# Narrow matmuls for the first modulation rows, another spread of the later ones, and the R loads on ScalarE's queue

## The chip, the core and the metric

The kernel runs on one core of a Trainium2 chip. A core has five engines, each of which executes its own instructions in order: TensorE (PE, with its weight loads as PEld), VectorE (DVE), ScalarE (ACT), GpSimd (POOL) and SyncE (SP), which here issues nearly all DMA transfers. An engine that meets an instruction whose inputs are not there waits, and everything behind it on that engine waits too. The metric is the device time of one execution in microseconds.

## The reference

One layer of a diffusion backbone with 128 context tokens and 2048 latent tokens, model width 1024. What matters here:

```python
shift1, scale1, gate1, shift2, scale2, gate2 = split(silu(c) @ w_mod + b_mod, 6)
h = rmsnorm(x, norm1) * (1 + scale1) + shift1
z = h @ w_in                      # conv parts, q, k, v, o and 16 gate columns
h_m = mlstm_bidir(q, k, v, gates, C0, n0, m0)      # chunks of 128 tokens, both directions
h_m = rmsnorm_per_head(h_m) * mh_norm * sigmoid(o)
x = x + gate1 * (concat(y_shortconv, h_m) @ w_out)
h2 = rmsnorm(x, norm2) * (1 + scale2) + shift2
x = x + gate2 * (ffn(h2) @ w_down)
```

The modulation is a vector of 6 x 1024 numbers for each of two conditionings (context and latent tokens), so w_mod is a 1024 x 6144 matrix that is multiplied by two columns. Shift1 and scale1 (the first 2048 numbers) are needed before any product of the layer; the other four parts are needed later.

## The kernel before

Data are kept transposed, 128 channels on the partitions and tokens along the free axis. Every large fp32 product is made of three matmuls: each operand x is split into a rounded part xH and a rest xL, and wh\*xH, wl\*xH and wh\*xL are accumulated. The split of a weight block costs one ScalarE copy (L112) and two VectorE subtractions (L115), for a block loaded by L110 into one of two buffers `wst`; the split of activations costs one ScalarE copy (L594) and one VectorE subtraction (L595) per tile.

A framework's scheduler turns the program into one instruction list per engine. It takes the instructions roughly in the order in which the code emits them and moves those that it expects to be ready sooner; so the place of a call in the code sets, within bounds, its place on each engine. Pools of a few buffers delay a load until the last user of the buffer is done.

The stages that the change touches:

- **Opening (0 to about 98 us).** `mod_pe` (L619 to L630) computes one row of 128 modulation numbers on TensorE: it loads a 512 KB block of w_mod (L625) into a free buffer of the tiles wsu or xg, multiplies it in 8 matmuls by the two conditioning columns, repeated to 128 columns (L628), and VectorE adds the bias to the first two columns (L630). `mods` does two rows (scale and shift) per 128 channels and then forms the factor `ab` (L120). `raws(0)` loads the first 512 latent tokens, `gsquares` (L582 to L591) adds up their squares (ScalarE L589, VectorE L590), `inv_rms` (L123 to L133) makes the inverse root mean square (TensorE L129, VectorE L132, GpSimd L133), `spread` (L140) copies it over the partitions, and `gapply` (L597 to L602) scales and shifts each tile (VectorE L600, ScalarE L601) and splits it. Then come the products of v and the gate columns, called vg (TensorE L397 to L399, evictions L402 and L404), 24 matmuls for each accumulator; there are four accumulator banks. `second` is the same for the next 512 tokens ("block 1") and runs beside the vg products of the first.
- **Pairs and first products (98 to 340 us)**, untouched.
- **Side rows.** The other 32 modulation rows are computed by VectorE: `mod_dve` loads a row block `wm` (L892) and does two multiply-and-sum instructions per row (L896) and one addition (L897). It is a generator that is advanced once at chosen places: at every second step of the vg products of the remaining tokens (loop L1204 to L1207), two rows for each step of the gate phase and each pair of k products (L1210 to L1219), at every second step of the woven sums (`weave`, L1184 to L1203), and the rest in a run behind them. The memory of `wm` is then given to the Mix units.
- **Gate phase (about 393 to 442 us).** `gate_phase` (L945 to L1033) turns the gate columns into decays: copies (L950), a minimum (L954, tile fe), exp and ln on ScalarE (L955, L956, each with a table load), a subtraction (L957, tile fc), transposes on TensorE (L964), scans over the tokens on VectorE (L914 to L939), and the transposed columns (L1001, TensorE L1003). The matmuls of the k heads (L216 to L218) run beside it.
- **Sums and Mix (about 440 to 960 us).** `weave` runs 34 units of the backward sums, then 34 units `Mix` (outputs), each a little beside large products as fill. A Mix unit loads R, a row of 1024 numbers broadcast to 128 partitions (512 KB, L1110, four buffers), adds the mask (VectorE L1122), takes exp (ScalarE L1126), makes the products (TensorE L1121, L1144, L1146; VectorE L1129, L1130), normalises (VectorE L1150 to L1154, ScalarE L1163 and L1167, TensorE L1173) and stores the gated result o (VectorE L1175, SP L1178). `out_proj` beside it loads rows of x (L485), multiplies by w_out, adds (VectorE L502), stores (L504) and squares (ScalarE L516, VectorE L517).
- Then the up and down products run until the end, on instruction lists that the change leaves alone.

Of the kernel before, what the change touches and what calls it, by code (L numbers as in the profile page):

```python
# [10 lines left out]
F32 = mybir.dt.float32  # L11
F32R = mybir.dt.float32r
AF = mybir.ActivationFunctionType
# [5 lines left out]
P = 128  # L19
# [24 lines left out]
def bc(ap, shape):  # L44
    return ap.to_broadcast(shape)
# [13 lines left out]
def hymba_kernel(ctx: ExitStack, tc: tile.TileContext, I, O):  # L59
    nc = tc.nc  # L60
    V, S, G, PE, Q = nc.vector, nc.scalar, nc.gpsimd, nc.tensor, nc.sync
# [30 lines left out]
    csil = cst.tile([P, KT, 2], F32, name="csil")  # L92
# [8 lines left out]
    ssp = ctx.enter_context(tc.tile_pool(name="ssp", bufs=2))  # L101

    def run(g, side=None, every=1):
        for i, _ in enumerate(g):
            if side and i % every == 0:
                next(side, None)
# [28 lines left out]
    def spread(r, n):  # L135

        ps = pst.tile([P, 512], F32, name="st")
        for i in range((n + P - 1) // P):
            w = min(P, n - i * P)
            PE.matmul(ps[:, i * P:i * P + w], bc(r[:w, i:i + 1], [w, P]), ident[:w, :w], start=True, stop=True)  # L140
        return ps
# [63 lines left out]
    def accumulator():  # L205
        pool = pa[next(turn_a) % len(pa)]
        return pool.tile([P, 512], F32, name="acc")
# [157 lines left out]
    with ExitStack() as ph1:  # L365
# [4 lines left out]
        sqp = ph1.enter_context(tc.tile_pool(name="sqp", bufs=2))  # L370
# [179 lines left out]
        with tc.tile_pool(name="ex", bufs=1, side="right") as ex, \  # L550
# [27 lines left out]
            def gcol(blk):  # L578
                c = TG // P + 4 * blk
                return rc[:, c:c + 4]  # L580

            def gsquares(xr):  # L582
                ss = ssp.tile([P, 512], F32, name="ss")
                for k, x in enumerate(xr):
                    if k == 0:
                        S.activation(ss, x, AF.Square)
                        continue
                    sq = sqp.tile([P, 512], F32, name="sq")
                    S.activation(sq, x, AF.Square)  # L589
                    V.tensor_add(ss, ss, sq)  # L590
                return ss  # L591

            def put(x, to):
                S.activation(to[0], x, AF.Copy)  # L594
                V.tensor_sub(to[1], x, to[0].bitcast(F32))  # L595

            def gapply(blk, xr):  # L597
                rb = spread(gcol(blk), NG)
                for k, x in enumerate(xr):
                    V.scalar_tensor_tensor(x, x, ab[:, 0, k, 1:2], rb[:, :NG], op0=ALU.mult, op1=ALU.mult)  # L600
                    S.activation(x, x, AF.Identity, bias=modT[:, k, 1:2])  # L601
                    put(x, plain[blk][k])  # L602
                    yield
# [16 lines left out]
            def mod_pe(mt):  # L620
                if next(homes6) == "u":
                    st = ex.tile([P, WN], F32, name="wsu", bufs=2)
                else:
                    st = xg.tile([P, 2, NG], F32, name="xg", bufs=4).rearrange("p k t -> p (k t)")
                Q.dma_start(st[:, :D], I["w_mod"][mt])  # L625
                ps = accumulator()
                for k in range(KT):
                    PE.matmul(ps[:, :P], st[:, k * P:(k + 1) * P], bc(csil[:, k, None, :], [P, 64, 2]),  # L628
                              start=(k == 0), stop=(k == KT - 1))
                V.tensor_scalar(modT[:, mt, :], ps[:, :2], bmod[:, mt:mt + 1], None, op0=ALU.add)  # L630

            def mods(k0, k1):
                for k in range(k0, k1):
                    mod_pe(8 + k)
                    mod_pe(k)
                    affine(0, k, k + 1)
# [6 lines left out]
            Q.dma_start(ident, I["ident"])  # L643
            mods(1, 2)
            x1 = raws(0)
            ss = gsquares(x1)
            mods(2, 4)
            ws = load_vg(0)
            inv_rms(ss, NG, gcol(0))
            mods(4, 8)  # L650
            run(gapply(0, x1))
            ws += load_vg(1)
            Q.dma_start(bgate, I["b_gate"].to_broadcast([P, 16]))
            x2 = raws(1)

            def second():
                ss = gsquares(x2)
                yield
                inv_rms(ss, NG, gcol(1))
                yield  # L660
                yield from gapply(1, x2)
# [5 lines left out]
            side = second()  # L667
# [6 lines left out]
            side = gsums(x1, x2)  # L674
# [187 lines left out]
            side = chain(first_stats(), prep_down())  # L862
# [39 lines left out]
        side = mod_dve()  # L902
# [194 lines left out]
        class Mix:  # L1097
# [6 lines left out]
            def load(self):  # L1104
                c, hp = self.c, self.hp
                self.k2, self.v2 = load2(ml, "k2", kD, c + 1, hp), load_v(c + 1, hp)
                self.q2 = load2(mb, "q2", qD, c + 1, hp)
                self.R = mb.tile([P, 2, 2, 2, P], F32, name="R", bufs=4)
                r0 = (c + 1) * H + 2 * hp
                Q.dma_start(self.R.rearrange("p h k d t -> p (h k d t)"),  # L1110
                            nD[r0:r0 + 2].rearrange("h k d t -> (h k d t)")[None, :].to_broadcast([P, 1024]))
                if c >= 0:
                    self.sb = ml.tile([P, 2, 2, 129], F32, name="sb", bufs=5)
                    Q.dma_start(self.sb, sD[hp, c])
# [65 lines left out]
        def weave(units, fill, blocks, lead, side=None):  # L1180

            n = len(units)
            for i in range(-1, n + 3):
                if 0 <= i < n:  # L1184
                    units[i].first()
                if 0 <= i - 3 < n:
                    units[i - 3].third()
                if 0 <= i - 1 < n:
                    units[i - 1].second()
                for x in range(lead) if i < 0 else (i + lead,):  # L1190
                    if x < n:
                        units[x].load()
                for _ in range(blocks[i % 3]):
                    next(fill, None)
                if side and i % 2:
                    next(side, None)


# [4 lines left out]

        for x, _ in enumerate(vg_first()):  # L1204
            next(third, None)
            if x % 2:
                next(side, None)  # L1207
        run(third)
        with tc.tile_pool(name="gt", bufs=1, side="right") as gt:
            gph = gate_phase()  # L1210
            kh = heads(BA, hs, 16, kD, AF.Copy, 1.0)
            while True:
                try:
                    next(gph)
                except StopIteration as e:
                    cols, colc, decB = e.value
                    break
                run(islice(kh, 2), side, 2)
            run(kh, side, 2)  # L1219
        sbs, sfs = [], []  # L1220
        for hp in range(2):
            sb = ml.tile([P, 2, 2, 129], F32, name="sb", bufs=5)
# [31 lines left out]
        side = sums(0, fpool, (0,), (6,))  # L1254
# [16 lines left out]
    with ph2:  # L1271
# [141 lines left out]
        side = sums(1, fpool)  # L1413
# [77 lines left out]
        for w, (hf, x) in enumerate(PRODS):  # L1491
            n = HN[hf] // 2 // NP[hf]
            for mp, ps in units_of(w):
                acc = {p: bank(next(turn))[:, :n] for p in ps}
                for c, nk in enumerate(KS):
# [4 lines left out]
                    for p in ps:  # L1500
                        for kk in range(nk):
                            k = slice(kk * P, (kk + 1) * P)
                            t = slice((NP[hf] * kk + p) * n, (NP[hf] * kk + p + 1) * n)
# [8 lines left out]
                    if jobs and jobs[0][0] + 1 <= step:  # L1512
                        k, ch = jobs[0]
# [93 lines left out]
```

## Time and profile before

| | |
|---|---|
| time, median of 3 runs | 2476.62 us (2476.61 to 2480.12) |
| profiled execution | 2481.01 us, of which the span is 2479.2 |
| TensorE busy | 2427.5 us (98%) |
| VectorE, ScalarE, GpSimd busy | 1806.6, 1146.3, 65.4 us |
| memory traffic | 506.08 MB, 204 GB/s mean |
| mean granted TensorE clock | 0.991 |

A row of a timeline has the start, the time, the engine, the line, the operation with its output and inputs, and in brackets the idle time of the engine before it and what ended that. A window's row has the busy time of each engine in that stretch and the granted clock of TensorE (1.00 is full). Lines are those of the kernel before; in the changed kernel the lines of the opening are one lower, and those from the side rows on are seven higher (L628 is L627, L896 is L903, L1110 is L1117).

### The profile page before, as it was taken

The numbers are of one execution on the slowest core, as the hardware profiler recorded it, in microseconds if no ns is written. First come the engines' busy times: TensorE is split into PE (matmuls) and PEld (weight loads), VectorE is DVE, ScalarE is ACT, GpSimd is POOL, SyncE is SP. The second block draws the span as 40 slices with busy tenths as digits, with TensorE's granted clock in tenths as the row PEclk, the third lists the DMA queues.
The fourth block names the chain that finished last, engine by engine and source line by source line (L and its number), as shares of the span: only waits on it lengthen the run. The fifth ranks groups of instructions, "written<-read, shape, count | busy, mean of one in ns | idle before, by whom it ended". The sixth has DMA issues, their size and how long they took to land.

```text
span 2479.2 us, 42907 instructions
## 1 busy us (share of the span) xinstructions
PE 2427.5 (98%) x16347; PEld 2322.7 (94%) x16347; DVE 1806.6 (73%) x3419; ACT 1146.3 (46%) x2166; POOL 65.4 (3%) x127
## 2 busy tenths in 40 slices
PE   8999999999999999999999999999999999999998
PEld 7987889989999989999999999999999988889998
DVE  4767678862567776888798879776767787677665
ACT  4533453352344444465454446555545554543343
POOL 0000000000101110000000000000000000000000
PEclk9999999999999999999999999999999999999999
DMA  7457557787567886966465446544444486576444
GB/s 287 129 191 256 206 191 223 234 257 217 163 190 232 280 249 197 302 233 234 143 229 195 164 143 240 185 149 161 138 161 145 164 292 221 201 275 208 173 155 149
DMA packets 249119, 506.08 MB, mean 204 GB/s; under 512 B 22722, under 2 KB 143698, under 8 KB 238034
## 3 DMA queue, kind: packets, MB, share of 16 engines
q1 hardware_dynamic: 248914, 503.35, 61.0%
q8 instruction: 128, 2.10, 0.4%
q14 instruction: 77, 0.63, 0.1%
HBM read 355.24 MB, written 148.03 MB: 203 GB/s over the span
## 4 chain that ended last, share of the span: by engine, by line
PE 78%; DMA 11%; DVE 7%; issue 2%; ACT 1%; SPq 1%; POOL 0%; DVEq 0%; ACTq 0%; POOLq 0%
PE pa L1446 7%; PE pa L1448 7%; PE pa L1447 7%; PE acc L216 4%; PE acc L218 4%; PE acc L217 4%; PE pb L1448 3%; PE pb L1446 3%; PE pb L1447 3%; PE pa L1505 2%; PE pa L1504 2%; PE pa L1506 2%; PE pc L1446 2%; PE pc L1448 2%; PE pc L1447 2%; DMA wm<-in_w_modr 2%
## 5 line engine op out<-in xcount | busy, mean ns | idle before, releaser
L1446 PE MATMUL pa<-tH,wh 128*128 128x272 f32 x1408 | 409.1, 291 | 3.1 <-DVE row L502 2.3
L1448 PE MATMUL pa<-tH,wl 128*128 128x272 f32 x1408 | 408.3, 290 | 0.0
L1447 PE MATMUL pa<-tL,wh 128*128 128x272 f32 x1408 | 406.3, 289 | 0.3 <-DVE tL L283 0.3
L289 ACT ACTIVATE wh<-st 128x512 fp32r<-128x512 f32 (+1 forms) x312 | 189.5, 609 | 412.8 <-PE pa L1447 117.2
L216 PE MATMUL acc<-hH,wh 128*128 128x384 f32 (+1 forms) x960 | 330.4, 344 | 0.0
L218 PE MATMUL acc<-hH,wl 128*128 128x384 f32 (+1 forms) x960 | 322.0, 335 | 0.0
L217 PE MATMUL acc<-hL,wh 128*128 128x384 f32 (+1 forms) x960 | 321.2, 335 | 0.0
L1287 DVE SCALAR_TENSOR_TENSOR tt<-raw,fw,tt 128x127 f32<-128x127 f32 (+4 forms) x264 | 242.3, 948 | 43.5 <-ACT tt L1293 42.3
L290 DVE TENSOR_TENSOR wl<-st,wh 128x512 fp32r<-128x512 f32 (+1 forms) x312 | 205.4, 661 | 92.8 <-ACT wh L289 88.9
L1446 PEld LDWEIGHTS pa<-tH,wh 128*128 128x128 f32 x1408 | 265.9, 189 | 3.9 <-DVE row L502 2.4
L1447 PEld LDWEIGHTS pa<-tL,wh 128*128 128x128 f32 x1408 | 266.7, 189 | 0.5 <-DVE tL L283 0.5
L1448 PEld LDWEIGHTS pa<-tH,wl 128*128 128x128 f32 x1408 | 265.6, 189 | 0.0
L1446 PE MATMUL pb<-tH,wh 128*128 128x272 f32 x704 | 204.0, 290 | 1.9 <-ACT tH L282 1.1
L1448 PE MATMUL pb<-tH,wl 128*128 128x272 f32 x704 | 203.8, 290 | 0.0
L1447 PE MATMUL pb<-tL,wh 128*128 128x272 f32 x704 | 202.9, 288 | 0.0
L216 PEld LDWEIGHTS acc<-hH,wh 128*128 128x128 f32 x960 | 182.0, 190 | 1.4 <-issue 0.4
L217 PEld LDWEIGHTS acc<-hL,wh 128*128 128x128 f32 x960 | 181.7, 189 | 0.8
L218 PEld LDWEIGHTS acc<-hH,wl 128*128 128x128 f32 x960 | 181.5, 189 | 0.4 <-issue 0.2
L289 ACT ACTIVATE wh<-s 128x512 fp32r<-128x512 f32 x176 | 110.9, 630 | 150.5 <-PE pc L1447 90.5
L290 DVE TENSOR_TENSOR wl<-s,wh 128x512 fp32r<-128x512 f32 x176 | 120.8, 687 | 32.1 <-ACT wh L289 28.3
L1446 PEld LDWEIGHTS pb<-tH,wh 128*128 128x128 f32 x704 | 132.6, 188 | 2.5 <-ACT tH L282 1.3
L1447 PEld LDWEIGHTS pb<-tL,wh 128*128 128x128 f32 x704 | 132.9, 189 | 0.1
(301 smaller groups left out, 5931.9 us busy)
## 6 DMA issues: line engine op xcount, KB each, us to landing
st<-in_w_up SPq DMA_DIRECT2D x88, 512.0 KB, 4.7
wU<-s SPq DMA_DIRECT2D x22, 1024.0 KB, 7.6
s<-wU SPq DMA_DIRECT2D x22, 1024.0 KB, 5.5
st<-wD SPq DMA_DIRECT2D x32, 704.0 KB, 4.2
st<-in_w_down SPq DMA_DIRECT2D x28, 704.0 KB, 4.2
wst<-in_w_in SPq DMA_DIRECT2D x38, 512.0 KB, 4.6
R<-nD SPq DMA_DIRECT2D x34, 512.0 KB, 5.0
wm<-in_w_modr SPq DMA_DIRECT2D x32, 512.0 KB, 4.9
```

The lines of the kernel that those rows point to most:

```text
L216: PE.matmul(acc[:, :n], w_h, hH[:, k, :n], start=(k == 0), stop=False)
L217: PE.matmul(acc[:, :n], w_h, hL[:, k, :n], start=False, stop=False)
L218: mm = PE.matmul(acc[:, :n], w_l, hH[:, k, :n], start=False, stop=(k == KT - 1))
L289: S.activation(wh[:, :n], a, AF.Copy)
L290: V.tensor_sub(wl[:, :n], a, wh[:, :n].bitcast(F32))
L1287: V.scalar_tensor_tensor(o, i, w, o, op0=ALU.mult, op1=ALU.add)
L1446: PE.matmul(acc, wh[:, w], rh, start=(kk == 0 and i in (0, 1, 5)), stop=False, skip_group_check=True)
L1447: PE.matmul(acc, wh[:, w], rl, start=False, stop=False, skip_group_check=True)
L1448: mm = PE.matmul(acc, wl[:, w], rh, start=False, stop=(kk == 3), skip_group_check=True)
L1504: PE.matmul(acc[p], wh[:, k], th[:, t], start=(c == kk == 0), stop=False, skip_group_check=True)
L1505: PE.matmul(acc[p], wh[:, k], tl[:, t], start=False, stop=False, skip_group_check=True)
L1506: PE.matmul(acc[p], wl[:, k], th[:, t], start=False, stop=(c == 2 and kk == nk - 1), skip_group_check=True)
```

## The change

Four edits:

1. The modulation matmuls move 32 columns instead of 128. The first two of them are used, as before.
2. `gsquares` becomes a generator. The squares of the first block are spread over modulation steps 2 to 4, the weights of vg are loaded and the inverse root follows, and `gapply(0)` is spread over steps 6 and 7.
3. R is loaded by ScalarE's DMA queue instead of SP's.
4. Side rows: 7 beside the vg products, none beside the gate phase and the k products, and in the woven sums at three of four steps instead of every second.

```diff
--- before.py
+++ after.py
@@ -579,16 +579,15 @@
                 c = TG // P + 4 * blk
                 return rc[:, c:c + 4]
 
-            def gsquares(xr):
-                ss = ssp.tile([P, 512], F32, name="ss")
+            def gsquares(xr, ss):
                 for k, x in enumerate(xr):
                     if k == 0:
                         S.activation(ss, x, AF.Square)
-                        continue
-                    sq = sqp.tile([P, 512], F32, name="sq")
-                    S.activation(sq, x, AF.Square)
-                    V.tensor_add(ss, ss, sq)
-                return ss
+                    else:
+                        sq = sqp.tile([P, 512], F32, name="sq")
+                        S.activation(sq, x, AF.Square)
+                        V.tensor_add(ss, ss, sq)
+                    yield
 
             def put(x, to):
                 S.activation(to[0], x, AF.Copy)
@@ -625,7 +624,7 @@
                 Q.dma_start(st[:, :D], I["w_mod"][mt])
                 ps = accumulator()
                 for k in range(KT):
-                    PE.matmul(ps[:, :P], st[:, k * P:(k + 1) * P], bc(csil[:, k, None, :], [P, 64, 2]),
+                    PE.matmul(ps[:, :32], st[:, k * P:(k + 1) * P], bc(csil[:, k, None, :], [P, 16, 2]),
                               start=(k == 0), stop=(k == KT - 1))
                 V.tensor_scalar(modT[:, mt, :], ps[:, :2], bmod[:, mt:mt + 1], None, op0=ALU.add)
 
@@ -643,18 +642,26 @@
             Q.dma_start(ident, I["ident"])
             mods(1, 2)
             x1 = raws(0)
-            ss = gsquares(x1)
-            mods(2, 4)
+            ss = ssp.tile([P, 512], F32, name="ss")
+            sq = gsquares(x1, ss)
+            for k in range(2, 5):
+                mods(k, k + 1)
+                run(islice(sq, 3))
             ws = load_vg(0)
             inv_rms(ss, NG, gcol(0))
-            mods(4, 8)
-            run(gapply(0, x1))
+            mods(5, 6)
+            ap = gapply(0, x1)
+            for k in range(6, 8):
+                run(islice(ap, 3))
+                mods(k, k + 1)
+            run(ap)
             ws += load_vg(1)
             Q.dma_start(bgate, I["b_gate"].to_broadcast([P, 16]))
             x2 = raws(1)
 
             def second():
-                ss = gsquares(x2)
+                ss = ssp.tile([P, 512], F32, name="ss")
+                run(gsquares(x2, ss))
                 yield
                 inv_rms(ss, NG, gcol(1))
                 yield
@@ -1107,7 +1114,7 @@
                 self.q2 = load2(mb, "q2", qD, c + 1, hp)
                 self.R = mb.tile([P, 2, 2, 2, P], F32, name="R", bufs=4)
                 r0 = (c + 1) * H + 2 * hp
-                Q.dma_start(self.R.rearrange("p h k d t -> p (h k d t)"),
+                S.dma_start(self.R.rearrange("p h k d t -> p (h k d t)"),
                             nD[r0:r0 + 2].rearrange("h k d t -> (h k d t)")[None, :].to_broadcast([P, 1024]))
                 if c >= 0:
                     self.sb = ml.tile([P, 2, 2, 129], F32, name="sb", bufs=5)
@@ -1192,7 +1199,7 @@
                         units[x].load()
                 for _ in range(blocks[i % 3]):
                     next(fill, None)
-                if side and i % 2:
+                if side and i % 4:
                     next(side, None)
 
 
@@ -1203,7 +1210,7 @@
 
         for x, _ in enumerate(vg_first()):
             next(third, None)
-            if x % 2:
+            if x < 14 and x % 2:
                 next(side, None)
         run(third)
         with tc.tile_pool(name="gt", bufs=1, side="right") as gt:
@@ -1215,8 +1222,8 @@
                 except StopIteration as e:
                     cols, colc, decB = e.value
                     break
-                run(islice(kh, 2), side, 2)
-            run(kh, side, 2)
+                run(islice(kh, 2))
+            run(kh)
         sbs, sfs = [], []
         for hp in range(2):
             sb = ml.tile([P, 2, 2, 129], F32, name="sb", bufs=5)
```

Three places show how this moves the instruction lists. First TensorE in the opening (L628/L627 modulation rows, L129 and L140 the inverse root and its spread, L397 to L399 vg), before:

```order
L628 MATMUL acc<-csil,wsu 128x128 x16
L628 MATMUL acc<-csil,xg 128x128 x32
L628 MATMUL acc<-csil,wsu 128x128 x16
L129 MATMUL st<-ones,ss 128x1 x4
L628 MATMUL acc<-csil,xg 128x128 x32
L628 MATMUL acc<-csil,wsu 128x128 x16
L628 MATMUL acc<-csil,xg 128x128 x16
L140 MATMUL st<-ident,rc 128x128 x4
L397 MATMUL acc<-wh,hH 128x264
```

and of the change:

```order
L627 MATMUL acc<-csil,xg 128x32 x8
L140 MATMUL st<-ident,rc 128x128 x2
L627 MATMUL acc<-csil,wsu 128x32 x8
L140 MATMUL st<-ident,rc 128x128 x2
L627 MATMUL acc<-csil,wsu 128x32 x8
L627 MATMUL acc<-csil,xg 128x32 x32
L627 MATMUL acc<-csil,wsu 128x32 x8
L397 MATMUL acc<-wh,hH 128x264
L398 MATMUL acc<-wl,hH 128x264
L399 MATMUL acc<-wh,hL 128x264
```

The spread of block 0 stands between rows 6 and 8 instead of behind all 16, and vg begins behind 13 rows; the other three rows stand between vg matmuls. Block 1's L140 has 115 vg matmuls ahead of it before, and 127 now.

Second VectorE ahead of the gate phase, from the eviction (L404) that runs at 391.67 us in the profile before (L896/L903 and L897/L904 are a side row, L115 the weight split, L954/L961 makes fe, L957/L964 fc). Before:

```order
L404 TENSOR_TENSOR gates<-acc,bgate 128x8
L896 SCALAR_TENSOR_TENSOR wm,mt<-wm,cB 128x1024
L950 COPY ic<-gates 128x64
L950 COPY fc<-gates 128x64
L897 TENSOR_SCALAR modT<-mt,bmod 128x2
L115 TENSOR_TENSOR wl<-wst,wh 128x512 x2
L896 SCALAR_TENSOR_TENSOR wm,mt<-wm,cB 128x1024
L404 TENSOR_TENSOR gates<-acc,bgate 128x8
L896 SCALAR_TENSOR_TENSOR wm,mt<-wm,cB 128x1024
L115 TENSOR_TENSOR wl<-wst,wh 128x512
```

and of the change:

```order
L404 TENSOR_TENSOR gates<-acc,bgate 128x8
L115 TENSOR_TENSOR wl<-wst,wh 128x512
L957 COPY ic<-gates 128x64
L957 COPY fc<-gates 128x64
L115 TENSOR_TENSOR wl<-wst,wh 128x512 x3
L903 SCALAR_TENSOR_TENSOR wm,mt<-wm,cB 128x1024
L404 TENSOR_TENSOR gates<-acc,bgate 128x8
L904 TENSOR_SCALAR modT<-mt,bmod 128x2
L903 SCALAR_TENSOR_TENSOR wm,mt<-wm,cB 128x1024 x2
L404 TENSOR_TENSOR gates<-acc,bgate 128x8
```

Four L115 now stand together ahead of the first side row of this stretch; up to fe there are four L903 where there were six L896.

Third ScalarE in Mix, around the load R that SP issues at 889.03 us before (L1126/L1133 is the exp, L516 the squares of out_proj, L1163/L1170 the sum of squares of the next outputs), of the change:

```order
L112 ACTIVATE wh<-wst 128x1024
L516 ACTIVATE sq<-row 128x384
L1133 ACTIVATE R<-R,cols 128x128 x4
L516 ACTIVATE sq<-row 128x384
L1117 DMA R<-nD 128x1024
L1170 ACTIVATE sj,hss<-hv 128x128 x2
L1174 ACTIVATE hv<-hv,hss 128x128 x2
```

The load stands between the second L516 and the L1170; before, the same ScalarE rows followed each other without it, and SP issued it behind a load of x and the store of o. Other R loads stand in the same way ahead of an L1170, mostly behind an L112 and an L516.

## The prediction

> **What bounds the kernel now.** I read the busy shares and the chain that ended last, then TensorE's waits by stage, then the stages that have them.
>
> ```profile
> PE 2427.5 (98%) x16347; PEld 2322.7 (94%) x16347; DVE 1806.6 (73%) x3419; ACT 1146.3 (46%) x2166; POOL 65.4 (3%) x127
> PE 78%; DMA 11%; DVE 7%; issue 2%; ACT 1%; SPq 1%; POOL 0%; DVEq 0%; ACTq 0%; POOLq 0%
> ```
>
> TensorE is busy for 98% of the span, so the kernel ends when its matmuls end, and all that the change can win is in the idle 50 us or in matmuls that run at a lower clock. The waits of TensorE, from the windows 0:60, 335:560 and 560:1080 (total, times, longest):
>
> ```profile
> PE acc L628 <- DVE ss L590: 3.3, 1, 3.3
> PE acc L397 <- ACT hH L594: 2.6, 1, 2.6
> ...
> PE S L964 <- DVE fc L957: 3.4, 1, 3.4
> PE S L1063 <- ACT kT L1065: 2.2, 2, 1.8
> PE S L1003 <- DVE cols L1001: 1.2, 1, 1.2
> ...
> PE st L129 <- DVE o L1175: 4.6, 1, 4.6
> ...
> PE st L1173 <- DVE rc L132: 1.1, 1, 1.1
> ```
>
> The change touches three of these places: the opening (L397), the gate phase (L964) and the outputs around 900 us (L129 behind o). A stall there costs more than its own length:
>
> ```profile
> 19.60:21.60 2.00, 2.00 (x11) 2.00 (x11) 0.78 (x3) 0.00 (x0) 0.00 (x0) 0.50 1.02 418
> 25.60:27.60 2.00, 2.00 (x20) 2.00 (x19) 1.74 (x6) 0.00 (x0) 0.00 (x0) 1.00 1.03 414
> 410.00:412.00 2.00, 2.00 (x7) 1.58 (x7) 2.00 (x7) 0.00 (x0) 0.00 (x0) 0.50 0.93 333
> 414.00:416.00 2.00, 2.00 (x11) 2.00 (x11) 1.90 (x8) 0.00 (x0) 0.00 (x0) 0.83 0.37 135
> 535.00:537.00 2.00, 2.00 (x13) 2.00 (x12) 2.00 (x5) 0.28 (x1) 0.00 (x0) 1.00 0.91 250
> 900.00:920.00 20.00, 18.49 (x101) 18.10 (x102) 17.05 (x54) 10.21 (x29) 4.94 (x6) 0.76 0.85 258
> ```
>
> (Columns: window, length, busy and count of PE, PEld, DVE, ACT and POOL, granted clock, DMA share, GB/s.) After the stalls of 3.3 and 3.4 us the granted clock is 0.50 and a window holds 11 passes for 20, or 7 for 11; behind the 1.8 of L1063 (at 533.5) it is 1.00. After 4.63 us at 900 the mean over 20 us is 0.76, which is 4.8 us of full clock lost.
>
> **The opening.** Today all 16 modulation rows run ahead of the first vg matmul, and the block's scaling starts when they end.
>
> ```profile
> 17.64 5.44 PE L628 MATMUL acc<-csil,xg 128*128 128x128 f32 x32 [3.27 <-DVE ss L590]
> 26.65 0.79 PE st L129 x8
> 27.43 14.40 PE acc L628 x128
> 41.83 0.91 PE st L140 x8
> 36.51 0.22 DVE L630 TENSOR_SCALAR modT<-acc,bmod 128x2 f32<-128x2 f32 x1 [1.57 <-PE acc L628]
> 45.36 0.39 PE L397 MATMUL acc<-wh,hH 128*128 128x264 f32 x1 [2.63 <-ACT hH L594]
> 62.69 1.71 PE st L140 x8
> 54.93 0.24 PE acc L399 x2
> ```
>
> Narrowing itself: a pass of 128 columns takes 14.40/128 = 0.1125 us, one of a single column 0.79/8 = 0.099, so 32 columns save 0 to 0.0135 us in each of 256 passes, 0 to 3.4 us in all. I take 0: the passes sit close to the one-column row, so the weight load sets them.
>
> By the Trainium skill (TensorE: Matmul & The Clock Gate, section LDWEIGHTS (loading the stationary operand)) a load of 128 columns takes about 107 ns whatever moves behind it; by that figure the 256 passes would save about 1.4 us. The rows agree as far as they reach.
>
> Moving: in the changed order vg starts behind row 13 of 16. Row 13 is evicted at 36.51 now; with the block's L140 (0.91) ahead of it and the scaling of the first tiles done beside the rows, I estimate vg at 38.7, not 45.36, and without the 2.63 stall and its half clock. The three rows left (16 passes of 0.1125 = 1.8 us each, 5.4) now stand among the vg matmuls. What gates the stage is its end, block 1's L140 at 62.69: its squares wait for x2 and, on ScalarE, stand behind the first vg evictions. 127 vg matmuls are ahead of it now, not 115; at 0.24/2 = 0.12 each that is 15.3, and with 5.4 TensorE is there at 59.4. That is 3.3 early, with 12 matmuls (1.45) more done: 4.7 at most. If the squares' chain stays where it is, only the 1.45 remains. I take -3.3, as the chain too begins earlier, but DVE has all its old work in it; ends -1.4 and -4.7, and another -2.6 if the rows before vg do get narrower in time.
>
> **The gate phase.** Side rows leave it: of the six L896 between the eviction at 391.67 and fe, four are left.
>
> ```profile
> L896 DVE SCALAR_TENSOR_TENSOR wm<-wm,cB 128x1024 f32<-128x1024 f32 x9 | 11.0, 1222 | 1.0 <-DMA wm<-in_w_modr 1.0
> 399.14 0.33 SPq L110 DMA_DIRECT2D wst<-in_w_in  x1
> 404.32 0.30 DVE L954 SCALAR_TENSOR_TENSOR fe<-fc 128x136 f32<-128x136 f32 x1
> 404.11 1.06 ACT L112 ACTIVATE wh<-wst 128x1024 fp32r<-128x1024 f32 x1 [3.70 <-DMA wst<-in_w_in]
> 405.19 1.28 ACT L955 ACT_TABLE_LOAD   x1
> 408.83 0.30 DVE L957 SCALAR_TENSOR_TENSOR fc<-fc,fe 128x136 f32<-128x136 f32 x1 [1.75 <-ACT fe L956]
> 409.19 0.47 PE L964 MATMUL S<-ident,fc 128*128 128x128 f32 x1 [3.39 <-DVE fc L957]
> ```
>
> ScalarE is the later of the two inputs: its weight rounding L112 waits for a load issued at 399.14, when the L115 pair before freed the buffer. In the changed order four L115 stand together ahead of the first of those rows, so this load can go some 3.5 us earlier, and L112 ends near 401.4; fe, with 2 x 1.22 plus two accumulator reads of 0.08 less ahead of it, is at 404.32 - 2.6 - 0.2 (an eviction row) or so, so the first table load runs right behind L112 and exp starts near 402.8. From exp to L964 it is 409.19 - 406.47 = 2.7 now, so L964 could go at 405.5; TensorE is there at 409.19 - 3.39 = 405.8. So the 3.39 goes nearly whole (I take 3.1), and with it the half clock: 17 passes at 2.00/7 = 0.29 instead of 2.00/11 = 0.18 are 1.9. L1003's 1.17 may go as well (two L896 fewer on its way), which I leave as an end. Sum 5.0, which I take, ends -2 (half the stall stays, and so the clock) and -7.
>
> **Side rows in the sums.** The last row ends three units of Sums later, and ScalarE's first R load waits for it because it takes its memory. ScalarE waits at that place now, too:
>
> ```profile
> 530.57 1.28 ACT L1126 ACTIVATE R<-R,colc 128x128 f32<-128x128 f32 x4 [4.43 <-DVE R L1122]
> ```
>
> so a 3 us wait lies in the 4.43; behind it stand L112, the eviction L412 and L1065, whose own lateness costs TensorE 2.2 above. Four more table loads fall here (4 x 1.28 on an engine busy for 46%). I take 0, ends -2 and +4.
>
> **R on ScalarE's queue.** 34 loads of 512 KB; DVE waits for them, TensorE only where its fill runs out.
>
> ```profile
>   DVE R L1122: 53.7, 24
> 887.07 0.33 SPq L485 DMA_DIRECT2D row<-in_x  x1
> 889.03 0.42 SPq L1110 DMA_DIRECT2D R<-nD  x1
> 884.96 0.53 ACT L516 ACTIVATE sq<-row 128x384 f32<-128x384 f32 x1 [0.90 <-DVE row L502]
> 887.56 0.31 ACT L1163 ACTIVATE sj<-hv 128x128 f32<-128x128 f32 x1 [2.08 <-DVE hv L1154]
> 894.05 0.69 DVE L1122 TENSOR_TENSOR R<-R,maskN 128x512 f32<-128x512 f32 x1 [4.87 <-DMA R<-nD]
> 900.37 1.44 PE L129 MATMUL st<-ones,ss 128*128 128x1 f32 x6 [4.63 <-DVE o L1175]
> 867.59 1.06 ACT L112 ACTIVATE wh<-wst 128x1024 fp32r<-128x1024 f32 x1 [3.34 <-DMA wst<-in_w_out]
> ```
>
> At the 4.63 stall, R went out at 889.03 because SP stood until 887.07 for a row buffer and issued three transfers ahead of it. On ScalarE it stands between the L516 that ends at 885.49 and the L1163 at 887.56: 3.5 us earlier. DVE's wait of 4.87 shrinks to 1.4, its string up to o moves by 3.5, and TensorE's stall is about 1.2; a stall of 1.8 left the clock at 1.00, so the 4.8 goes as well if nothing comes next. What comes next is the 1.14 of L1173 and a stage whose DMA share is 0.85, so I count the 3.4 whole and 1.1 of the 4.8: -4.5. The other R near the end keep their time within 0.3 by the same reading of the two orders. Ends: -8.2, and +3 if a load lands behind a blocked L112 (below).
>
> The Trainium skill (DMA: Bandwidth & Descriptors, section Issuing engines are not separate DMA queues) says that another issuing engine gives no bandwidth, only issue time. No run here shows the first part; by it the gain is just that of a load that was late on SP, which is how I counted it.
>
> **Sum**: -3.3 - 5.0 + 0 - 4.5 = -12.8. The profiled execution took 2481.0 us (span 2479.2 and 1.8 beside it), 4.4 over the median, 2476.62; so 2468.2 for it and **2463.8** for the median.
>
> **Rivals.**
> (a) Only one of the three places pays: block 1's squares still gate the opening (-1.4), and the 900 us stall changes owner, because L502's accumulator or the row loads are ready no sooner (0); with the gate's -5.0 and a little clock, 2476.6 - 6 = 2470.5. For it: DMA share 0.85 at 900. Against: DVE runs without a gap from 894.05 to the end of o.
> (b) All ends hold: -4.7 - 7 - 8.2 = -19.9, 2456.7. For it: each stall drops the clock. Against: each takes several conditions at once.
> (c) Slower: ScalarE is in order, so an R load behind an L112 that waits for its weights goes out when they land, which held it 3.34 us at 867.59. Where an R goes out more than some 1.2 us later than on SP, TensorE's stall passes 1.8 and costs its length and the clock: 4.6 + 4.8 = 9.4 at the size of 900.37. Two new ones, and none removed: +18.8 - 8.3 (opening, gate) = +10.5, 2487. Against: these R have stood at the times when L112 ended.
> (d) The narrow passes leave the clock at half. At 0.50 a pass takes 2.00/11 = 0.182, a row 2.9 for 1.8, twelve rows from 17.64 on +13.2; with -12.8 for the rest, 2477: no difference. For it: only a quarter of the columns stream. Against: the row of one-column passes ran at full clock, though for 0.8 us alone.
> The Trainium skill (TensorE: Matmul & The Clock Gate, section Part 1: The HAM clock gate) makes the clock depend on how busy the array was in a window of about 3.4 us; it does not say whether a weight load counts as busy, and this rival turns on that.
>
> **How the numbers follow.** Forecast 0.50, (a) 0.22, (b) 0.10, (c) 0.11, (d) 0.07. A measurement of this kernel tells about 0.2%, 5.0 us, from no change: bounds 2471.7 and 2481.6. Faster: 0.48 + 0.14 + 0.10 = 0.72; same: 0.02 + 0.08 + 0.06 = 0.16; slower: 0.01 + 0.11 = 0.12. The range reaches from (b) to the edge of no change: 2455 to 2479; (c) is left out.
>
> **What would show it.** Opening: the first L397 row near 39 and the L140 of block 1 near 60; a granted clock of 0.5 in the windows from 20 to 40 would be (d). Gate: L964's wait under 1.5 and clock 1.00 from 405 on. Outputs: the wait of L129 behind o under 2 and the clock of 900:920 near 0.95; L1122's waits larger than 53.7 with new TensorE stalls at L1121 or L129 would be (c). It is wrong if the three places gain less than 5 us together or a new stall over 2.5 us stands in 520 to 960.

## The result and the profile after

The change makes the kernel slower: 2501.88 us median of 5 runs (2497.82 to 2505.67) against 2476.62 us (2475.02 to 2480.12), a ratio of 1.0099 with a 95% interval of 1.0085 to 1.0112. The forecast was 2463.8, range 2455 to 2479. The span of the profiled execution is 2499.8 us, 20.6 above the one of before, which lay 4.4 over its median.

The waits of TensorE in the changed kernel look harmless (windows 0:60, 335:560 and 560:1080; L627 is L628 of the kernel before, L971 is L964, L1182 is L1175):

```profile
PE acc L627 <- DMA wsu<-in_w_mod: 6.0, 1, 6.0
PE st L129 <- DVE ss L589: 2.3, 1, 2.3
PE acc L397 <- DVE modT L629: 0.4, 1, 0.4
...
PE y L1081 <- DVE sb L1095: 2.9, 4, 1.3
PE S L971 <- DVE ls L972: 2.4, 1, 2.4
PE S L971 <- DVE fc L964: 0.5, 1, 0.5
...
PE st L129 <- DVE o L1182: 5.1, 1, 5.1
PE y L1081 <- DVE sb L1095: 3.7, 1, 3.7
PE S L1128 <- DVE R L1137: 3.0, 2, 1.6
```

The 2.6 and 3.4 us waits of before are gone or small. Yet the page of the profile has TensorE busier than before by 25 us:

```profile
PE 2452.3 (98%) x16347; PEld 2348.2 (94%) x16347; DVE 1808.7 (72%) x3419; ACT 1150.8 (46%) x2170; POOL 64.5 (3%) x127
```

The number of instructions is the same, 16347. So the same matmuls took longer, and the timeline of TensorE in the opening shows which:

```profile
5.96 7.00 PE L627 MATMUL acc<-csil,wsu 128*128 128x32 f32 x32 [5.96 <-DMA wsu<-in_w_mod]
12.77 10.43 PE L627 MATMUL acc<-csil,xg 128*128 128x32 f32 x48
...
39.15 13.84 PE L627 MATMUL acc<-csil,xg 128*128 128x32 f32 x64
52.80 3.60 PE L627 MATMUL acc<-csil,wsu 128*128 128x32 f32 x16
56.80 0.56 PE L397 MATMUL acc<-wh,hH 128*128 128x264 f32 x1 [0.41 <-DVE modT L629]
...
76.42 0.42 PE L397 MATMUL acc<-wh,hH 128*128 128x264 f32 x1
76.64 0.42 PE L398 MATMUL acc<-wl,hH 128*128 128x264 f32 x1
76.86 0.36 PE L399 MATMUL acc<-wh,hL 128*128 128x264 f32 x1
...
88.60 1.16 PE L140 MATMUL st<-ident,rc 128*128 128x128 f32 x8 [0.76 <-POOL rv L401]
```

A narrow pass takes 13.84/64 = 0.216 us, where a pass of 128 columns took 0.1125. The vg matmuls behind them start 0.22 us apart (76.42 to 76.64) and only from about 77 us on 0.12 apart. Up to there the opening ran at half speed, and block 1's L140 stands at 88.60 instead of 62.69. Of these 25.9 us, 1.45 were given back by the 12 vg matmuls that are done earlier; 24.5 are lost.

Now the trap. The windows of the changed kernel give a granted clock of 1.00 for this time:

```profile
26.00:30.00 4.00, 4.00 (x21) 4.00 (x20) 0.23 (x2) 0.00 (x0) 1.01 (x1) 1.00 0.20 80
78.00:82.00 4.00, 4.00 (x35) 4.00 (x34) 1.72 (x5) 3.12 (x7) 0.12 (x2) 1.00 0.27 85
```

21 passes in 4 us beside a clock of 1.00, where full clock gave 40 (20 in 2.00 us in the row of before). In this trace the clock's first record lies at the rise near 77 us; what was ahead of it is shown as 1.00. Busy time was no help either: TensorE is 100% busy in both rows. The count of instructions in a window, or the time of one, told the state; the clock column didn't. The prediction's sign for (d), a granted clock of 0.5 in the windows from 20 to 40, can't be seen here for the same reason.

Behind the opening the difference stays near 23 us for 300 us (the first matmul of L682, now L689, starts at 121.7 and not 98.4), falls to 19.7 at the gate phase (428.9 for 409.2), and rises to 24.4 in the sums (L1121, now L1128, begins at 645.7 for 621.3).

### The profile page after: what moved, and what is told of

Its sections match the earlier page's. It is cut to its first block, busy times and chain, and to the rows that moved or that the text cites. A ratio compares the mean times of both kernels' runs of the same rounds, so it can differ in the third digit from the quotient of the medians.

```text
span 2499.8 us, 42932 instructions
## 1 busy us (share of the span) xinstructions
PE 2452.3 (98%) x16347; PEld 2348.2 (94%) x16347; DVE 1808.7 (72%) x3419; ACT 1150.8 (46%) x2170; POOL 64.5 (3%) x127
## 4 chain that ended last, share of the span: by engine, by line
PE 81%; DMA 9%; DVE 6%; issue 2%; ACT 1%; POOL 0%; SPq 0%; DVEq 0%; ACTq 0%; POOLq 0%
PE pa L1453 7%; PE pa L1455 7%; PE pa L1454 7%; PE acc L216 5%; PE acc L218 5%; PE acc L217 4%; PE pb L1455 3%; PE pb L1453 3%; PE pb L1454 3%; PE pa L1511 2%; PE pa L1512 2%; PE pa L1513 2%; PE acc L627 2%; DMA wm<-in_w_modr 2%; PE pc L1454 2%; PE pc L1455 2%
```

## The experiments

**The width, taken back.** Theory: narrow passes leave TensorE at half clock. Rival: the new order of the opening costs.

```diff
-                    PE.matmul(ps[:, :32], ..., bc(csil[:, k, None, :], [P, 16, 2]),
+                    PE.matmul(ps[:, :P], ..., bc(csil[:, k, None, :], [P, 64, 2]),
```

> The changed kernel with the modulation matmuls moving 128 columns again; everything else of the change stays. Theory (the narrow passes leave TensorE at half clock, so that each costs 0.216 us instead of 0.1125): the whole loss of the opening goes; block 1's L140 stands near 60 to 62 us instead of 88.6, and the time is 2474 to 2480 us (2501.9 less 23 to 26). What is left over the prediction's 2463.8 is then the price of its other terms. Rival (the new order of the opening costs, the width is harmless): 2495 us or more, and passes of 0.2 us stay.

Measured: 2471.02 us against 2474.44, ratio 0.9983 (0.9972 to 0.9994). The opening of this run:

```profile
22.76 3.73 PE L627 MATMUL acc<-csil,wsu 128*128 128x128 f32 x32
26.33 3.73 PE L627 MATMUL acc<-csil,xg 128*128 128x128 f32 x32
...
57.18 1.16 PE L140 MATMUL st<-ident,rc 128*128 128x128 f32 x8 [0.75 <-POOL rv L401]
```

32 passes in 3.6 us again, and the L140 is 5.5 us earlier than in the kernel before, also earlier than the expected 60 to 62; the time is 3 us under the expected range. The width alone decides the sign of the change. One reservation: the width also moves the scheduler. With 128 columns vg begins behind all 16 rows, not behind 13. The run with 96 columns below answers it.

**The width alone**, put into the kernel before.

```diff
-                    PE.matmul(ps[:, :P], ..., bc(csil[:, k, None, :], [P, 64, 2]),
+                    PE.matmul(ps[:, :32], ..., bc(csil[:, k, None, :], [P, 16, 2]),
```

> The kernel before with only the width changed to 32 columns. Theory (half clock): 256 passes at 0.216 instead of 0.1125 us, less the 3 us that start at half clock anyway, so the first vg matmul stands near 66 us instead of 45.36 and its first 5 us run at half clock: +20 to +26, 2496 to 2503 us. Rival (order costs, width is harmless): 2473 to 2480 us.

Measured: 2501.48 against 2474.44, ratio 1.0107 (1.0092 to 1.0123). This one edit is worth the whole loss. Its TensorE list in the opening is that of the changed kernel (vg behind 13 rows), so the order that the prediction put down to the spread of `gsquares` and `gapply` comes from the narrow width. The first vg matmul stands at 56.28 (expected near 66, which left the three rows out that stand behind it).

**How narrow is too narrow?**

```diff
-                    PE.matmul(ps[:, :32], ..., bc(csil[:, k, None, :], [P, 16, 2]),
+                    PE.matmul(ps[:, :64], ..., bc(csil[:, k, None, :], [P, 32, 2]),
```

> The changed kernel with 64 columns. If the clock follows the share of time in which columns stream and the bound lies between 32 and 64: like 128 columns, 2474 to 2480 us. If it lies between 64 and 128: like 32 columns, 2498 to 2506 us and passes of 0.216 us. A value between them would mean that the clock changes within the opening. Rival (order costs): no change, 2498 to 2506 us.

Measured: 2495.25 against 2474.44, ratio 1.0079 (1.0063 to 1.0095), passes of 0.216 us: half clock as with 32 columns. It is 3 us under the range that was expected for that; two narrow rows and not three stand among the vg matmuls, and block 1's L140 comes at 81.19, not 88.60. Then 96 columns, and 128 and 32 in turn:

```diff
-                    PE.matmul(ps[:, :32], ..., bc(csil[:, k, None, :], [P, 16, 2]),
+                    PE.matmul(ps[:, :96], ..., bc(csil[:, k, None, :], [P, 48, 2]),
```

> The changed kernel with 96 columns. The runs so far put the bound of the clock between 64 columns (passes of 0.216 us, 2495) and 128 (0.112, 2471). If it lies under 96: passes of 0.11 us after the first 4 us and 2469 to 2474 us. If over 96: passes of 0.216 us and 2490 to 2497 us.

```diff
-                    PE.matmul(ps[:, :32], ..., bc(csil[:, k, None, :], [P, 16, 2]),
+                    n = 32 if k % 2 else P
+                    PE.matmul(ps[:, :n], ..., bc(csil[:, k, None, :], [P, n // 2, 2]),
```

> The changed kernel with matmuls of 128 and 32 columns in turn (a mean of 80). If what counts is the share of the time in which columns stream over some us: the side of the bound on which 80 lies, one state throughout (2469 to 2474 or 2490 to 2502 us), and together with the run of 96 columns it narrows the bound. If single wide passes were enough to raise the clock: 2469 to 2474 us whatever 96 columns give.

Measured: 2478.44 against 2473.37 with 96 (ratio 1.0027, 1.0014 to 1.0041), 2483.81 in turn (1.0048, 1.0032 to 1.0064). Rows of 64 columns, of 96, and of the kernel in turn a window and three rows (a merged row is named by its first matmul; L628 is L627 there):

```profile
39.62 10.34 PE L627 MATMUL acc<-csil,xg 128*128 128x64 f32 x48
```

```profile
22.72 3.74 PE L627 MATMUL acc<-csil,wsu 128*128 128x96 f32 x32
26.30 3.74 PE L627 MATMUL acc<-csil,xg 128*128 128x96 f32 x32
58.11 1.69 PE L140 MATMUL st<-ident,rc 128*128 128x128 f32 x8 [0.76 <-POOL rc L133]
```

```profile
35.00:40.00 5.00, 5.00 (x25) 5.00 (x25) 0.45 (x3) 0.00 (x0) 1.01 (x1) 1.00 0.45 160
...
41.58 2.05 PE L140 MATMUL st<-ident,rc 128*128 128x128 f32 x8
43.42 4.24 PE L628 MATMUL acc<-csil,xg 128*128 128x128 f32 x32
47.50 3.74 PE L628 MATMUL acc<-csil,wsu 128*128 128x128 f32 x32
```

With 96 columns the clock rises and a pass takes 0.112 us, as with 128; with 64 it does not. The bound for rows of one width lies between 64 and 96 columns. The run with 96 also answers the reservation above: vg begins behind 14 rows there, and L140 still stands at 58.11. So an order that leaves rows among the vg matmuls is not what costs 26 us.

With 128 and 32 columns in turn (a mean of 80) the rows stay at half clock for 36 us, 25 passes in 5 us. Behind the eight passes of 128 columns that spread the inverse root (L140) the clock rises, and then rows in turn run at full clock: 32 passes in 3.74 us. So the mix did not raise the clock, but held it once it was up. One state throughout, as expected, was wrong, and 2483.81 lies between the two ranges.

The time with 96 columns is 4 us over the expected 2469 to 2474, and that isn't explained. The wait of L129 behind o at 900 us, 8.3 us, is no longer than the 8.8 with 128 columns. In this profile the clock falls once more at block 1's L140 (0.50 from 58.6 to 61.9), where with 128 columns it stays at 1.00. Three of the ten runs took 2484 to 2489 us at a mean granted clock of 0.988 or 0.989, the other seven 2475 to 2480 at 0.990 to 0.992; there is no trace of those three. Whether 96 columns always hold the clock stays open.

**Does a clock that is up stay up?** The kernel before, its first eight rows wide and the last eight narrow:

```diff
+                    n = P if mt in (8, 0, 9, 1, 10, 2, 11, 3) else 32
-                    PE.matmul(ps[:, :P], ..., bc(csil[:, k, None, :], [P, 64, 2]),
+                    PE.matmul(ps[:, :n], ..., bc(csil[:, k, None, :], [P, n // 2, 2]),
```

> The kernel before with the first eight modulation rows at 128 columns (the clock is full by then) and the last eight at 32. If narrow passes count as an idle array, the clock falls about 3.4 to 7 us after the last wide row and the other passes take 0.216 us: +6 to +12, 2483 to 2489 us. If the clock, once full, holds as long as instructions follow without a gap: passes stay at 0.1 to 0.11 us, 2473 to 2479 us, and the lesson is only not to start with narrow passes.

Measured: 2486.35 against 2474.44, ratio 1.0045 (1.0027 to 1.0062): the clock falls, and the time is the expected one. Here the fall lies behind the first record, so that the clock column can be read:

```profile
27.42 1.95 PE L629 MATMUL acc<-csil,xg 128*128 128x32 f32 x16
30.03 2.35 PE L629 MATMUL acc<-csil,xg 128*128 128x32 f32 x16
33.18 6.87 PE L629 MATMUL acc<-csil,xg 128*128 128x32 f32 x32
...
30.00:32.00 2.00, 2.00 (x18) 2.00 (x16) 0.00 (x0) 0.00 (x0) 0.00 (x0) 0.81 0.89 311
34.00:36.00 2.00, 2.00 (x11) 2.00 (x11) 0.83 (x2) 1.76 (x3) 0.00 (x0) 0.50 1.01 401
```

The first narrow row still runs at full clock, and its passes start 0.112 us apart, as wide ones do: at one clock the width makes no difference. Some 4.5 us after the last wide row the clock is at 0.50. TensorE had been idle for 0.11 us in that time, and among the narrow passes stood only eight of one column (L129) and four of 128 (L140). To whatever sets the clock, narrow passes count for little. This is the direct proof of the cause: TensorE busy, clock down. The order of the opening is not that of the kernel before (vg begins behind 13 rows again), but the fall comes 12 us ahead of the first vg matmul.

**R's queue.** First the changed kernel with 128 columns and R on SP, then the kernel before with only R moved.

```diff
-                S.dma_start(self.R.rearrange("p h k d t -> p (h k d t)"),
+                Q.dma_start(self.R.rearrange("p h k d t -> p (h k d t)"),
```

> The changed kernel with 128 columns and with R on SP's queue again, so only the opening's order and the side rows' places are left of the change. Theory (on ScalarE the R loads go out no earlier where it matters, and ScalarE stands still behind a load that may not be issued yet): the wait of L129 behind o falls from 8.8 us to the 4.6 to 5.7 of the kernels with R on SP, and the 3.2 at the handover from the sums shrinks too: 2463 to 2468 us, 3 to 8 under the 2471.0 with R on ScalarE. Rival (R's queue does not matter, the stall at 900 us depends on the phase of the loads): 2469 to 2473 us and a stall of 8 us or more stays.

```diff
-                Q.dma_start(self.R.rearrange("p h k d t -> p (h k d t)"),
+                S.dma_start(self.R.rearrange("p h k d t -> p (h k d t)"),
```

> The kernel before with only R moved to ScalarE's queue. Theory: slower by 3 to 8 us, 2477 to 2483, with a longer wait of L129 behind o than 4.6 us. Rival (no matter): within 2 us of the kernel before, 2472 to 2477. The prediction's step would make it faster by 4.5, 2470.

Measured: 2467.77 against 2474.32, ratio 0.9975 (0.9962 to 0.9989) without the move; 2478.66 against 2474.32, ratio 1.0022 (1.0011 to 1.0034) with the move alone. The move alone costs 4.3 us (2.7 to 8.4 by the interval). With 128 columns the version with R on ScalarE has the ratio 0.9983, the one with R on SP 0.9975; this points the same way, but the intervals overlap. ScalarE, VectorE and TensorE around the R load in question, in the kernel before with R on ScalarE's queue, with SP's row of the transfer that ended the wait:

```profile
878.64 0.53 ACT L516 ACTIVATE sq<-row 128x384 f32<-128x384 f32 x1 [0.89 <-DVE row L502]
886.67 0.33 ACTq L1110 DMA_DIRECT2D R<-nD  x1
887.04 0.31 ACT L1163 ACTIVATE sj<-hv 128x128 f32<-128x128 f32 x1 [7.88 <-DMA xt<-yD]
...
879.69 0.43 SPq L464 DMA_DIRECT2D xt<-yD  x1
...
891.32 0.69 DVE L1122 TENSOR_TENSOR R<-R,maskN 128x512 f32<-128x512 f32 x1 [8.46 <-DMA R<-nD]
...
898.11 1.44 PE L129 MATMUL st<-ones,ss 128*128 128x1 f32 x6 [7.63 <-DVE o L1175]
```

ScalarE was free at 879.17 and stood at R's issue for 7.5 us, by the profile until the 768 KB load of xt that SP had issued at 879.69 had landed; the sum of squares L1163 stood behind it. VectorE waits 8.46 us for R (4.87 in the kernel before) and TensorE 7.63 (4.63). Why R's issue has to wait for that load isn't shown: R's buffer isn't xt's. The size of TensorE's stall at this place varies: 4.2 to 7.2 us over the runs with R on SP, 5.1 in the changed kernel and 7.6 to 8.8 in the other runs with R on ScalarE. The times carry the verdict, the rows show one place.

**The side rows alone**, in the kernel before.

```diff
-                if side and i % 2:
+                if side and i % 4:
...
-            if x % 2:
+            if x < 14 and x % 2:
...
-                run(islice(kh, 2), side, 2)
-            run(kh, side, 2)
+                run(islice(kh, 2))
+            run(kh)
```

> The kernel before with only the side rows moved (7 beside vg, none beside the gate phase, three of four steps in the sums). The prediction's gate term alone would give -5, 2469 to 2470. From the trace of the change: the gate wait falls from 3.4 to 0.5 us, but L971's second transpose waits 2.0 to 2.4 us for ls, and the later last row delays the first R loads by 7 us: -3 for the gate and clock, 0 to +4 for the handover: 2471 to 2476 us. Rival (nothing is gained, the stall only moves): 2474 us or more.

Measured: 2471.32 against 2474.32, ratio 0.9992 (0.9981 to 1.0002): not told from no change. The gate's waits in this run:

```profile
407.18 0.33 PE L964 MATMUL S<-ident,fc 128*128 128x128 f32 x1 [0.43 <-DVE fc L957]
410.05 0.33 PE L964 MATMUL S<-ident,ic 128*128 128x128 f32 x1 [2.01 <-DVE ls L965]
```

The 3.39 in front of the first transpose is 0.43, but the second now waits 2.01 for the copy ls. In the changed kernel VectorE shows why:

```profile
428.58 0.30 DVE L964 SCALAR_TENSOR_TENSOR fc<-fc,fe 128x136 f32<-128x136 f32 x1 [0.38 <-ACT fe L963]
429.17 1.22 DVE L903 SCALAR_TENSOR_TENSOR wm<-wm,cB 128x1024 f32<-128x1024 f32 x1 [0.29 <-DMA wm<-in_w_modr]
430.44 1.22 DVE L903 SCALAR_TENSOR_TENSOR wm<-wm,cB 128x1024 f32<-128x1024 f32 x1
431.84 0.28 DVE L972 COPY ls<-S 128x128 f32<-128x128 f32 x1
```

Both halves of a side row stand between fc and ls, where the kernel before had one. The code advances no side row beside the gate phase any more, but rows from ahead of it still run there.

**The rows sooner.** In the changed kernel the first R load goes out at 551.50, right behind the last side row, and TensorE then waits 3.7 us for a sum (sb). To see whether the late row is to blame, a version on top of the 128 columns and SP's queue gets one row at every step of the sums:

```diff
-                if side and i % 4:
+                if side:
...
-            if x < 14 and x % 2:
+            if x % 2:
```

> As e5_wide_r_on_sp, but with 9 side rows beside vg as before and one at every step of the woven sums, so that the last row ends as early as before. If the late last row is what the handover costs: no wait of 3 us in the sums, 2 to 5 us under e5_wide_r_on_sp, 2460 to 2465 us. If not: the same as e5_wide_r_on_sp within 2 us, or slower by new waits in the sums where VectorE is full.

Measured: 2471.96 against 2474.32, ratio 0.9997 (0.9985 to 1.0009), 4 us above the version without it. That version had no long wait for sb to win back: its longest was 1.2 us, and it is 1.5 here. The wait for ls grew from 1.4 to 2.9, the longest for R from 2.2 to 3.5, and kT has 2.8 in total in both. The lateness of the last row isn't what is left to win.

**The opening's order alone**, in the kernel before:

```diff
+            sq = gsquares(x1, ss)
+            for k in range(2, 5):
+                mods(k, k + 1)
+                run(islice(sq, 3))
...
+            ap = gapply(0, x1)
+            for k in range(6, 8):
+                run(islice(ap, 3))
+                mods(k, k + 1)
+            run(ap)
```

> The kernel before with only the opening's new order (the squares and the scaling spread over the modulation steps), with 128 columns, R on SP and the side rows as before. If the parts add up: e5_wide_r_on_sp less e7_before_side is -3.5, so 2470 to 2472 us, with the opening's second L140 near 56 us instead of 62.7 and the gate wait of 3.4 us still there. If the opening carries the whole gain of e5_wide_r_on_sp: 2467 to 2469. If the gain is taken back later: 2473 or more.

Measured: 2469.27 against 2473.27, ratio 0.9986 (0.9973 to 0.9998); block 1's L140 is at 57.36, no wait of 2.63 stands in front of vg, and the gate wait is 3.7. The time lies between two of the ranges that were expected for it.

**A warm start.** With the clock in mind, ten matmuls of a constant ahead of the first row, while its data are on the way, on top of the version with 128 columns and R on SP:

```diff
+            pw = accumulator()
+            for _ in range(10):
+                PE.matmul(pw[:, :P], ones, ones, start=True, stop=True)
             mod_pe(8)
```

> As e5_wide_r_on_sp, with ten matmuls on a constant tile (their result is used by nothing) ahead of the first modulation row, while its data are on the way. If only the array's activity sets the clock: the first row's passes take 0.112 us at once (two rows in 3.6 us instead of 5.2 to 6.6), 2465 to 2467 us, 1 to 3 under e5_wide_r_on_sp. If the rows' data bound the opening anyway (the 2.7 us wait for xg grows by as much): no difference, within 1.5 us of e5_wide_r_on_sp.

Measured: 2471.19 against 2473.37, ratio 0.9986 (0.9973 to 0.9998): nothing gained over the version without them (0.9975), and the expected 2465 to 2467 was missed. The rows say why:

```profile
1.04 4.64 PE L640 MATMUL acc<-ones 128*128 128x128 f32 x20 [1.04 <-DVE mhalf L91]
5.46 4.59 PE L627 MATMUL acc<-csil,wsu 128*128 128x128 f32 x32
9.89 3.73 PE L627 MATMUL acc<-csil,xg 128*128 128x128 f32 x32
17.03 5.44 PE L627 MATMUL acc<-csil,xg 128*128 128x128 f32 x32 [3.41 <-DMA xg<-in_w_mod]
```

The first two rows take 4.59 us and not 5.2 to 6.6, and what is won is spent in the wait for the next block of weights, 3.41 us, behind which the clock is down again. The row behind that wait starts at 17.03, against 17.06 without the ten matmuls.

The best version that ran is the changed kernel with 128 columns and R on SP: 2467.77 us, 0.25% under the kernel before; its interval overlaps with that of the opening's order alone.

## Why the prediction was wrong

The step that failed is **"Narrowing itself: ... I take 0: the passes sit close to the one-column row, so the weight load sets them."** At one clock the width makes no difference, as the step said; what it left out is the clock. The eight one-column passes that carried the step stood among wide ones and were over in 0.8 us; a row of them is too short to show what 30 us of them do. Measured: 0.216 us a pass for 0.1125, and +27.0 us for the edit alone, where the step had 0 to -3.4. Rival (d) had this mechanism, with a chance of 0.07 and too small a price: 0.182 a pass for twelve rows of 16 (+13.2). The 0.182 is 2.00 us over a count of 11 that takes in the passes cut by the window's edges; the passes in that window start 0.21 us apart. With 0.216 for all of the 256 passes it is 256 x 0.1035 = 26.5. About 30 of the passes ran at half clock in the kernel before, too, so the passes alone come to some 23; the interval of the +27.0, 22.8 to 30.4, holds both.

The row that could have warned was in the same trace: the first passes of 128 columns, which start at half clock and need about 3 us until it rises. It showed that full speed is not given but earned, and the question was what earns it. The Trainium skill (TensorE: Matmul & The Clock Gate, section Part 1: The HAM clock gate) says that the clock follows how busy the array has been in a window of about 3.4 us. The runs agree in size, with 3 to 6 us from the first wide pass to the rise and some 4.5 us to the fall, and add what busy does not mean: the busy time of the profile, which was 100%.

**The opening** (-3.3): right in size, in part by luck. Measured alone it is -4.0 us (-6.7 to -0.5 by the interval), and the L140 came 5.3 us sooner. The 2.63 us stall ahead of vg and its half clock went, as worked out. But vg did not begin behind 13 rows; that order came from the narrow width.

**The gate phase** (-5.0): fc came as early as worked out (0.4 to 0.5 us of wait for 3.39). That the stall would move to ls was not foreseen, though it could have been counted in the order: two L903 between fc and the copy, one before. In the run with only the side rows moved, the whole edit is -3.0 us with an interval that holds zero.

**Side rows in the sums** (0, end +4): not settled. In the changed kernel R waits for its load on VectorE, a sum (sb) stands behind R, and TensorE waits 3.7 us for it, with a clock of 0.91 over 40 us:

```profile
568.40 0.69 DVE L1129 TENSOR_TENSOR R<-R,maskN 128x512 f32<-128x512 f32 x1 [4.75 <-DMA R<-nD]
...
570.61 1.23 PE L1081 MATMUL y<-vw,kT 128*128 128x258 f32 x2 [3.71 <-DVE sb L1095]
...
560.00:600.00 40.00, 36.12 (x189) 33.45 (x188) 16.44 (x36) 28.32 (x58) 0.00 (x0) 0.91 0.74 225
```

That takes two of the edits together. The longest wait for sb in the window 500:700 is 1.3 us with only the rows moved, 0.4 with only R moved, 1.2 with the rows moved and R on SP, and 2.2 to 3.7 in the five kernels that have both. What the rows cost there by themselves no run shows; gate and sums together are the -3.0.

**R on ScalarE's queue** (-4.5): wrong in sign, +4.3 us alone. The step "On ScalarE it stands between the L516 that ends at 885.49 and the L1163 at 887.56: 3.5 us earlier" took the place in the order for the time of issue. An issue also waits, here 7.5 us, by the profile for a load of SP's. Rival (c) had the shape, an in-order ScalarE that stands, but named a different wait.

**The stall that leaves the clock up.** The prediction took it from one place that a stall of 1.8 us leaves the clock at 1.00, and used it for this term and for rival (c). The length of a stall does not decide it. The same row in the versions with 128 columns, R on ScalarE and R on SP:

```profile
17.48 5.44 PE L627 MATMUL acc<-csil,xg 128*128 128x128 f32 x32 [1.85 <-DMA xg<-in_w_mod]
...
17.06 3.81 PE L627 MATMUL acc<-csil,xg 128*128 128x128 f32 x32 [2.71 <-DMA xg<-in_w_mod]
```

Behind 1.85 us of waiting the clock is at 0.50 (18.2 to 21.5), behind 2.71 us it stays at 1.00. In the kernel before it is at 0.50 from 63.2 to 66.4, behind waits of 0.28 and 0.74 us.

Added up, the four edits measured alone give +27.0 - 4.0 - 3.0 + 4.3 = +24.3; the change gave +25.3, the same within the noise of the parts.

## What to carry to other kernels

Don't make a long run of matmuls narrower to save columns. Where passes of 32 and 128 columns take the same time at one clock, nothing is saved, and at 64 columns and under the clock fell or never rose, which here doubled each pass and slowed what came behind for another 5 us. Read the clock's state from the spacing of equal matmuls, not from busy time, and not from the clock column ahead of its first record. And when a transfer is moved to another engine's queue, ask what its issue waits for, not only what stands in front of it.

## What the runs showed of the hardware that was not expected

- Passes of 32 and of 64 columns leave TensorE at half clock for as long as they run (0.216 us each; until 72 us in the changed kernel), passes of 96 and 128 don't (0.112 us). At full clock a pass of 32 columns takes 0.112 us, too.
- 128 and 32 in turn did not raise the clock in 36 us, but kept it up once it had risen.
- A clock at full speed falls some 4.5 us into a run of narrow passes, with 0.11 us of idle time in them.
- After narrow passes the wide vg matmuls take about 5 us to raise the clock (72.10 to 77 us in the changed kernel).
- A wait of 1.85 us was followed by half clock, one of 2.71 us at the same place in another run was not.
- A DMA issue on ScalarE stood 7.5 us, by the profile until a transfer issued by SP had landed, and held ScalarE's computing with it.
